# A two-layer hybrid encoder on one core: the delta rule's inverses by smaller blocks stored by row, and roots and gates by ScalarE's logarithm

## The chip, the core and the metric

The kernel runs on one core of one Trainium2 chip. The core has TensorE (matrix products, into PSUM), VectorE and GpSimd (elementwise work and reductions), ScalarE (activation functions, copies with a scale) and SyncE, whose queue starts the transfers of weights. Each engine takes its instructions in order and waits on semaphores for the others. The metric is the device time of one execution in microseconds; the median of three runs before the change is 1150.33 us (1150.1 to 1151.57). Less is better.

## The reference

256 tokens of width 1024 go through two layers. A layer is a gated feed-forward part of width 2752, a mixer and a second feed-forward part, each after an RMS norm; a last norm follows.

```python
for l in range(DEPTH):
    x = x + 0.5 * swiglu(rms_norm(x, ln_ffn1[l]), ffn1_w_in[l], ffn1_w_out[l])
    h = rms_norm(x, ln_mix[l])
    x = x + hybrid_mixer(h, ...)          # window attention, differential attention, gated delta rule
    x = x + 0.5 * swiglu(rms_norm(x, ln_ffn2[l]), ffn2_w_in[l], ffn2_w_out[l])
return rms_norm(x, ln_final)
```

The mixer has six window-attention heads, four differential heads and six heads of a gated delta rule that runs forward and backward over chunks of 64 tokens. For the delta rule each chunk, head and direction needs a triangular solve, and its decay comes from a softplus:

```python
g = -jnp.exp(a_log) * jax.nn.softplus(dn_a + dt_bias)
m_low = where(tril_strict, einsum(kb, kc) * decay, 0)     # 64 x 64
a_mat = eye(64) + m_low
u = triangular_solve(a_mat, vb);  w = triangular_solve(a_mat, kb * exp(gc))
```

With 4 chunks, 6 heads and 2 directions there are 48 unit-triangular matrices of 64 x 64 in a layer. All norms are of the form `v * rsqrt(mean(v*v) + 1e-6)`.

## The kernel before

The state `x` stays on chip with its 1024 channels on partitions, as 8 blocks of 128 x 256 tokens. Feed-forward parts multiply in three passes (`mm3`, L259 to L261): ScalarE splits off a high part of each 128 x 1024 weight block (`load`, L253), VectorE the remainder (L254). The mixer multiplies 32-bit weights directly (`proj`, L428; `token_proj`, L439; `out_proj`, L1024).

The mixer is cut into pieces; the text `ORDER` lists them as they are written into the program. From it the framework plans each engine's queue: it works with priorities in this order and its own idea of when inputs are ready, so the instructions of neighbouring pieces interleave. Weights are fetched on SyncE's queue seven blocks ahead, in the order of the pieces that read them. PSUM has three pools of banks (`BANK`); projections ("pj"), attention scores ("pss"), the gate's projection ("pz") and the output projection ("py") share the two of pool "pm", so a projection or a score waits until a bank has been read out.

The pieces that matter here:

- `N` (`norm`, `norm_scale`): TensorE sums the squares, VectorE forms mean plus EPS (L204), `rsqrt` gives the root, TensorE spreads it over partitions ("pb"). `rsqrt` (L159 to L176) starts from an integer trick and makes three Newton steps, eleven small VectorE instructions. It also serves the feed-forward parts' norms, the q and k norms (`qn`), the differential heads' norm (`dn`), the delta rule's output norm (`on`) and the last norm (`final`).
- `G` (`gates`): beta and g for 24 columns; the softplus term log(1 + e) is a series of 13 VectorE instructions (L466 to L475) after an exponential on ScalarE (L464).
- `c`, `co`, `ce`: nine convolutions, with a Tanh for the SiLU (L559). `qc`, `E`, `X`: decay and the products of k with k and q, into `XE`.
- `ic`, `i`, `ir`, `io`, `ie`: the inverse of the diagonal 32 x 32 blocks. Each partition holds one block; `Vi` and `L` are [128, 32 x 32]. `inv_start` brings the blocks into `L`. One step is a product of broadcast views into `pr` (L799) and a reduction over the last axis (L800). `inv_row` (`ir`) makes rows 1 to 15 of the two 16 x 16 diagonal blocks at once, reading `L` down columns; `inv_off` (`io:0` to `io:5`) makes the 16 x 16 block below. Four of these products, for rows 2, 4, 11 and step 4 (names in `SHARED`: v2, v4, v11, u4), are on GpSimd. `inv_end` transposes the inverse into place; `f` and `g` make the 64 x 64 inverse by products on TensorE.
- `p:9` to `p:16` (`att`), `d` (`diff_scores`), `w` (`win_scores`), `h`, `hw`: projections and attention. A differential head's scores need the maximum on VectorE (L716) and four exponentials on ScalarE (L719) before their two banks are free. They stand between the steps of the inverse in `ORDER`.
- `sa`, `sb`, `sc`: the scan over chunks. `ze`: the output gate, with a Tanh (L927). `on`, `oT`, `o`: output norm, transposes, output projection.

ScalarE's functions come in tables of which one is active; a table load stands in its queue wherever the next function isn't in the active one.

Of the kernel before, what the change touches and what calls it, by code (L numbers as in the profile page):

```python
# [16 lines left out]
P = 128  # L17
# [19 lines left out]
A:0 A:1 A:2 K N A:3 G V c:1:0 c:1:1 clear c:0:0 c:1:2 GS co:1:0 c:0:1 co:1:1 co:1:2 ce:1 GE GT E:1 qn:1 co:0:0 co:0:1  # L37
# [15 lines left out]
SHARED = set("O2 S2 d0 d1 d2 d3 g5 s3 t1 t7 t8 u4 v11 v2 v4 x0 x4 x5".split())  # L53
# [4 lines left out]
class Kernel:  # L58
# [104 lines left out]
    def rsqrt(self, v, n, name, out=None):  # L163

        nc, sp = self.nc, self.sp
        ti = sp.tile([P, n], I32, tag=f"rs_i{n}", name=f"{name}_i")
        nc.vector.tensor_scalar(ti, v.bitcast(I32), 1, None, ALU.arith_shift_right)
        y = sp.tile([P, n], F32, tag=f"rs_y{n}", name=f"{name}_y")
        nc.vector.tensor_scalar(y.bitcast(I32), ti, -1.0, float(0x5F3759DF), ALU.mult, ALU.add)
        a = sp.tile([P, n], F32, tag=f"rs_a{n}", name=f"{name}_a")  # L170
        for i in range(3):
            nc.vector.scalar_tensor_tensor(a, v, -0.5, y, ALU.mult, ALU.mult)
            nc.vector.tensor_tensor(a, a, y, ALU.mult)
            o = y if i < 2 or out is None else out
            nc.vector.scalar_tensor_tensor(o, a, 1.5, y, ALU.add, ALU.mult)
        return o  # L176
# [16 lines left out]
    def norm_scale(self, name, last=False):  # L193
# [12 lines left out]
        self.rsqrt(v, 2, name, rt)  # L206
# [57 lines left out]
    def ffn(self, l, i, gnext, first):  # L264
# [3 lines left out]
        with tc.tile_pool(name=f"hp{nm}", bufs=1) as hp, tc.tile_pool(name=f"ht{nm}", bufs=3) as ht:  # L268
# [19 lines left out]
            for j in range(NF):  # L288
# [34 lines left out]

            c0 = NF * 2048 + 1024
# [30 lines left out]
    def mixer(self, l, gnext):  # L355
# [22 lines left out]
        with ExitStack() as ctx:  # L378
# [74 lines left out]
            def gates():  # L453
# [11 lines left out]
                z1 = tile_([P, 2, 24], "z1")  # L465
                ts(z1, ab, 2.0, None, ALU.add)  # L466
                nc.vector.reciprocal(z1, z1)
                tt(z1, z1, ab, ALU.mult)
                z2 = tile_([P, 2, 24], "z2")
                tt(z2, z1, z1, ALU.mult)  # L470
                sr = tile_([P, 2, 24], "sr")
                ts(sr, z2, 2.0 / 17, None, ALU.mult)
                for m in (15, 13, 11, 9, 7, 5, 3):
                    stt(sr, sr, 2.0 / m, z2, ALU.add, ALU.mult)
                stt(sr, sr, 2.0, z1, ALU.add, ALU.mult)  # L475
# [104 lines left out]
            def qk_norm(a):  # L580

                raw = st["raw", a]
                sqt = tile_([P, 2, 384], "sqt2", "pr")
                act(sqt, raw, AF.Square)
                ss = tile_([P, 12], f"ss{a}")
                nc.vector.tensor_reduce(ss, sqt.rearrange("p t (h d) -> p (t h) d", d=64), AX.X, ALU.add)
                ts(ss, ss, EPS, None, ALU.add)
                rq = self.rsqrt(ss, 12, f"{nm}qk{a}").rearrange("p (t h) -> p t h", t=2)
                if a == 0:
                    ts(rq, rq, 0.125, None, ALU.mult)  # L590
                for p in range(2):
                    v_ = heads6(raw[:, p, :])
                    tt(v_, v_, rq[:, p, :].unsqueeze(2).to_broadcast([P, 6, 64]), ALU.mult)
# [169 lines left out]
            def diff_norm():  # L763
# [6 lines left out]
                r = self.rsqrt(hv, 8, f"{nm}dn").rearrange("p (a h) -> p a h", a=2)  # L770
# [53 lines left out]
            def inv_row(i0, i1):  # L824
                Vi, L = st["Vi"], st["L"]
                for i in range(i0, i1):
                    products(
                        blk(Vi, i, (528, 2), (32, i)),
                        blk(L, i, (528, 2), (0, i), (32, i)),
                        blk(Vi, 0, (528, 2), (32, i), (1, i)),  # L830
                        (2, i, i),
                        True,
                        f"v{i}",
                    )

            def inv_off(n):
                Vi, L, pp = st["Vi"], st["L"], st["pp"]
                if n < 2:
# [3 lines left out]
                        blk(L, 16 + i0, (1, 8), (0, 8), (32, 16)),  # L842
# [175 lines left out]
            def out_proj(part, d):  # L1018
# [20 lines left out]
                "clear": clear, "N": norm, "V": values, "G": gates, "GS": gate_sums, "GE": gate_exps, "GT": gate_rows,  # L1039
                "c": conv, "co": conv_out, "ce": conv_end, "qn": qk_norm, "qc": qk_channels,  # L1040
                "E": decay, "X": products_kq, "K": constants, "p": att, "hw": win_out, "w": win_scores, "d": diff_scores, "h": head_out,
                "dn": diff_norm, "oT": to_oT, "ic": inv_clear, "i": inv_start, "ir": inv_row, "io": inv_off, "ie": inv_end,
# [193 lines left out]
```

## Time and profile before

| what | value |
|---|---|
| median of 3 runs | 1150.33 us |
| profiled execution, its own time | 1153.34 us |
| its span, first to last instruction | 1151.5 us |
| TensorE busy | 1110.3 us, 96% |
| VectorE busy | 738.0 us, 64% |
| ScalarE busy | 522.9 us, 45% |
| GpSimd busy | 82.3 us, 7% |
| mean granted clock of TensorE | 0.977 |
| read from HBM | 171.17 MB |

A share of busy time is a mean over stages with different limits. Matmuls are pipelined and their ends are modelled, so a busy TensorE is not TensorE at its peak: at a lower granted clock the same instructions count as more busy time. In rows of groups the columns are line, engine, operation, result and operands with shapes, count, busy us, mean ns of one, and the idle time before them with what ended it. Rows of the timeline have start, length, engine, line, operation, and in brackets the idle time before and its releaser. PE is TensorE, DVE VectorE, ACT ScalarE, POOL GpSimd, SP SyncE.

### The profile page before, as it was taken

What the parts mean: (1) busy time and instruction counts of PE and PEld (TensorE: products, weight loads), DVE (VectorE), ACT (ScalarE), POOL (GpSimd) and SP (SyncE); (2) the same over time, 40 slices, a digit from 0 to 9 for tenths busy, and PEclk for the clock granted to TensorE, in tenths of its full rate; (3) what the DMA queues carried; (4) which work ended last, traced back from release to release, by engine and by line L of the source; (5) the groups of instructions that cost most, each with busy time, mean ns of one, the idle gap of its engine ahead of it and who ended that gap; (6) DMA issues with size and microseconds to landing.
All of it is one profiled execution on the core that took longest, in us unless ns stands there. A gap on an engine that the chain in (4) does not pass through costs nothing. (4 is left out here: it accounts for less than half of the span.)

```text
span 1151.5 us, 21957 instructions
## 1 busy us (share of the span) xinstructions
PE 1110.3 (96%) x8970; PEld 1022.2 (89%) x8970; DVE 738.0 (64%) x1442; ACT 522.9 (45%) x967; POOL 82.3 (7%) x135
## 2 busy tenths in 40 slices
PE   7999999998899999999999999999988999999996
PEld 7999999776668999999999999988756689999996
DVE  7766654778747566666566666547786476666653
ACT  5545442263472454454444454415436435445441
POOL 0000011101201200000100000121020021000010
PEclk9999999998899999999999999999988999999998
DMA  9655653521123555565555565534211254556521
GB/s 332 213 182 186 201 168 115 164 77 53 51 61 111 198 174 181 184 202 184 181 180 183 182 199 184 161 125 128 79 50 37 75 184 155 185 184 203 184 97 37
DMA packets 49637, 173.64 MB, mean 151 GB/s; under 512 B 5504, under 2 KB 6784, under 8 KB 49536
## 3 DMA queue, kind: packets, MB, share of 16 engines
q1 hardware_dynamic: 49104, 171.64, 45.5%
q8 instruction: 70, 1.15, 0.4%
q10 hardware_dynamic: 432, 0.60, 0.1%
q14 instruction: 31, 0.25, 0.1%
HBM read 171.17 MB, written 1.05 MB: 150 GB/s over the span
## 5 line engine op out<-in xcount | busy, mean ns | idle before, releaser
L254 DVE TENSOR_TENSOR wl<-wr,wh 128x1024 fp32r<-128x1024 f32 x254 | 311.7, 1228 | 172.5 <-ACT wh L253 172.0
L259 PE MATMUL ps<-xh,wh 128*128 128x256 f32 x1336 | 379.6, 284 | 0.8 <-ACT wh L253 0.8
L261 PE MATMUL ps<-xh,wl 128*128 128x256 f32 x1336 | 379.0, 284 | 0.8 <-DVE wl L254 0.8
L253 ACT ACTIVATE wh<-wr 128x1024 fp32r<-128x1024 f32 x254 | 267.2, 1053 | 246.6 <-issue 144.6
L260 PE MATMUL ps<-xl,wh 128*128 128x256 f32 x1336 | 378.7, 283 | 0.0
L259 PEld LDWEIGHTS ps<-xh,wh 128*128 128x128 f32 x1336 | 257.1, 192 | 1.6 <-ACT wh L253 1.0
L261 PEld LDWEIGHTS ps<-xh,wl 128*128 128x128 f32 x1336 | 257.0, 192 | 1.2 <-DVE wl L254 1.2
L260 PEld LDWEIGHTS ps<-xl,wh 128*128 128x128 f32 x1336 | 257.1, 192 | 0.0
L261 PE MATMUL ps<-hh,wl 128*128 128x256 f32 x672 | 187.9, 280 | 0.0
L260 PE MATMUL ps<-hl,wh 128*128 128x256 f32 x672 | 187.7, 279 | 0.0
L259 PE MATMUL ps<-hh,wh 128*128 128x256 f32 x672 | 187.6, 279 | 0.0
L428 PE MATMUL pj<-xf,wr 128*128 128x256 f32 x544 | 133.6, 402 | 2.9 <-issue 2.6
L260 PEld LDWEIGHTS ps<-hl,wh 128*128 128x128 f32 x672 | 126.3, 188 | 0.0
L261 PEld LDWEIGHTS ps<-hh,wl 128*128 128x128 f32 x672 | 126.1, 188 | 0.0
L259 PEld LDWEIGHTS ps<-hh,wh 128*128 128x128 f32 x672 | 125.9, 187 | 0.0
L428 PEld LDWEIGHTS pj<-xf,wr 128*128 128x128 f32 x544 | 107.6, 203 | 20.0 <-issue 3.3
L191 POOL TENSOR_TENSOR sqacc<-sqacc,sqt 128x256 f32<-128x256 f32 x41 | 34.6, 843 | 733.0 <-ACT sqt L187 732.9
L282 ACT ACTIVATE hh<-h 128x256 fp32r<-128x256 f32 x88 | 36.1, 416 | 90.4 <-DVE h L280 90.4
L277 DVE TENSOR_TENSOR t<-ps,f_rb 128x256 f32<-128x256 f32 x88 | 36.9, 424 | 37.9 <-PE ps L261 37.7
L1024 PE MATMUL py<-oT,wr 128*128 128x256 f32 x256 | 58.9, 384 | 0.0
L283 DVE TENSOR_TENSOR hl<-h,hh 128x256 fp32r<-128x256 f32 x88 | 36.8, 423 | 30.5 <-ACT hh L282 30.5
L1024 PEld LDWEIGHTS py<-oT,wr 128*128 128x128 f32 x256 | 47.2, 190 | 7.0 <-DVE x L1031 0.4
(321 smaller groups left out, 1128.5 us busy)
## 6 DMA issues: line engine op xcount, KB each, us to landing
wr<-in_ffn SPq DMA_DIRECT2D x258, 512.0 KB, 3.4
wr<-in_mix SPq DMA_DIRECT2D x50, 512.0 KB, 3.5
wr<-in_mix SPq DMA_DIRECT2D x8, 408.0 KB, 3.2
wr<-in_mix SPq DMA_DIRECT2D x8, 384.0 KB, 3.0
x<-in_x SPq DMA_DIRECT2D x4, 256.0 KB, 4.1
ar<-in_ffn SPq DMA_DIRECT2D x8, 128.0 KB, 3.9
cb<-in_constb SPq DMA_DIRECT2D x1, 588.0 KB, 10.1
out_y<-fo SPq DMA_DIRECT2D x2, 256.0 KB, 2.4
```

What stands on the lines that cost most here:

```text
L191: (eng or nc.gpsimd).tensor_tensor(self.sq, self.sq, t, ALU.add)
L253: nc.scalar.activation(h, w, AF.Copy)
L254: nc.vector.tensor_tensor(lo, w, h.bitcast(F32), ALU.subtract)
L259: mm(out, lhsT=ah, rhs=bh, start=start, stop=False)
L260: mm(out, lhsT=ah, rhs=bl, start=False, stop=False)
L261: mm(out, lhsT=al, rhs=bh, start=False, stop=stop)
L277: nc.vector.tensor_tensor(t[:rows], gate, rb[:rows], ALU.mult)
L282: nc.scalar.activation(hh[:n, j, :], h[:n], AF.Copy)
L283: nc.vector.tensor_tensor(hl[:n, j, :], h[:n], hh[:n, j, :].bitcast(F32), ALU.subtract)
L428: mm(ps[:, 0:S], lhsT=w[:, k * P : (k + 1) * P], rhs=xf[:, k, :], start=k == 0, stop=k == KD - 1)
L1024: mm(ps[:, 0:S], lhsT=st["o", q // NBLK][:, c], rhs=oT[:, k, :], start=k == ks[0], stop=k == ks[-1])
```

## The change

- **Inverse.** `ir` makes only rows 1 to 7, of four 8 x 8 diagonal blocks at once. Four new steps `im:0` to `im:3` (`inv_mid`) make the 8 x 8 block below each pair: per 16 x 16 block one step for L times the upper inverse into `pp`, one for the lower inverse times that. `io:0` to `io:5` stay, with `io:0` to `io:2` reading `L` by rows.
- **Layout.** `inv_start` transposes on VectorE the four groups that ScalarE copied before, and copies the other four, so that `L` is stored by row where it was stored by column.
- **GpSimd.** v2, v4, v11 and u4 leave `SHARED`: every product of the inverse is on VectorE.
- **Roots.** `rsqrt` takes `exp(-0.5 * ln(v))` on ScalarE and one Newton step on VectorE in the mixers' first norm, the output norm and the last norm; the feed-forward norms, `qn` and `dn` keep the old form.
- **Softplus.** `ln(1 + e)` is one activation on ScalarE in place of the series.
- **Tables.** `log_table` puts a load of the table with logarithm and exponential at the head of each mixer (`lt`), after `ze`, and in the last feed-forward part after its last hidden block. The load is queued behind the ScalarE instruction written before it.
- **Order.** `ORDER` loses `ir:8:9` to `ir:15:16` and gains `im:0` to `im:3` and the two `lt`.

```diff
-ir:3:4 ir:4:5 ir:5:6 p:15 ir:6:7 ir:7:8 ir:8:9 ir:9:10 ir:10:11 ir:11:12 ir:12:13 ir:13:14 c:2:2 ir:14:15 p:14 p:13
-co:2:0 p:16 d:0 ir:15:16 d:2 co:2:1 io:0 co:2:2 p:9 d:1 p:12 d:3 w:0 io:1 h:2 h:1 p:10 h:0 io:2 io:3 h:3 p:11 w:1 w:2
+ir:3:4 ir:4:5 ir:5:6 p:15 ir:6:7 ir:7:8 im:0 im:1 im:2 c:2:2 im:3 p:14 p:13 co:2:0 p:16 d:0 d:2 co:2:1 io:0 co:2:2 p:9
+d:1 p:12 d:3 w:0 io:1 h:2 h:1 p:10 h:0 io:2 io:3 h:3 p:11 w:1 w:2 hw:0 io:4 io:5 ie ce:2 dn hw:1 f g:0 hw:2 g:1 sa:0
...
-SHARED = set("O2 S2 d0 d1 d2 d3 g5 s3 t1 t7 t8 u4 v11 v2 v4 x0 x4 x5".split())
+SHARED = set("O2 S2 d0 d1 d2 d3 g5 s3 t1 t7 t8 x0 x4 x5".split())
...
-    def rsqrt(self, v, n, name, out=None):
+    def rsqrt(self, v, n, name, out=None, log=True):
...
+        if log:
+            nc.scalar.activation(y, v, AF.Ln)
+            nc.scalar.activation(y, y, AF.Exp, scale=-0.5)
+        else:
...
-        for i in range(3):
+        steps = 1 if log else 3
+        for i in range(steps):
...
+    def log_table(self):
+
+        self.tc.keep_in_program_order(self.nc.scalar.preload_act_table_set("natural_log_exp_and_others"))
...
-                    _, rb = self.norm_scale(nm)
+                    _, rb = self.norm_scale(nm, log=False)
...
+            if gnext is None:
+                self.log_table()
...
-                z1 = tile_([P, 2, 24], "z1")
-                ts(z1, ab, 2.0, None, ALU.add)
-                nc.vector.reciprocal(z1, z1)
-                tt(z1, z1, ab, ALU.mult)
-                z2 = tile_([P, 2, 24], "z2")
-                tt(z2, z1, z1, ALU.mult)
                 sr = tile_([P, 2, 24], "sr")
-                ts(sr, z2, 2.0 / 17, None, ALU.mult)
-                for m in (15, 13, 11, 9, 7, 5, 3):
-                    stt(sr, sr, 2.0 / m, z2, ALU.add, ALU.mult)
-                stt(sr, sr, 2.0, z1, ALU.add, ALU.mult)
+                act(sr, ab, AF.Ln, bias=1.0)
...
-                        if (b < 2) == (v == 0):
+                        if (b < 2) != (v == 0):
                             nc.vector.transpose(o_, XE[B32[b], 0, us, B32[b % 2]])
...
-                        blk(Vi, i, (528, 2), (32, i)),
-                        blk(L, i, (528, 2), (0, i), (32, i)),
-                        blk(Vi, 0, (528, 2), (32, i), (1, i)),
-                        (2, i, i),
+                        blk(Vi, i, (264, 4), (32, i)),
+                        blk(L, 32 * i, (264, 4), (0, i), (1, i)),
+                        blk(Vi, 0, (264, 4), (32, i), (1, i)),
+                        (4, i, i),
...
+            def inv_mid(n):
+
+                Vi, L, pp = st["Vi"], st["L"], st["pp"]
+                a, step = n % 2, n // 2
+                if step == 0:
+                    products(
+                        blk(pp, a * 64, (1, 8), (8, 8)),
+                        blk(L, a * 528 + 8 * 32, (32, 8), (0, 8), (1, 8)),
+                        blk(Vi, a * 528, (0, 8), (32, 8), (1, 8)),
+                        (8, 8, 8), False, f"m{n}",
+                    )
+                else:
+                    products(
+                        blk(Vi, a * 528 + 8, (1, 8), (32, 8)),
+                        blk(Vi, a * 528 + 264, (1, 8), (0, 8), (32, 8)),
+                        blk(pp, a * 64, (0, 8), (8, 8), (1, 8)),
+                        (8, 8, 8), True, f"m{n}",
+                    )
...
-                        blk(L, 16 + i0, (1, 8), (0, 8), (32, 16)),
+                        blk(L, (16 + i0) * 32, (32, 8), (0, 8), (1, 16)),
...
-                        blk(L, 16 + 8 * 32, (1, 16), (0, 8), (32, 8)),
+                        blk(L, 16 * 32 + 8, (32, 16), (0, 8), (1, 8)),
```

More of the change, by code (lines that the diff above doesn't have):

```diff
@@ L160, in psum @@
         return self.pools[tag].tile(shape, F32, tag=tag, name=name)
-    def rsqrt(self, v, n, name, out=None):
+    def rsqrt(self, v, n, name, out=None, log=True):
         nc, sp = self.nc, self.sp
-        ti = sp.tile([P, n], I32, tag=f"rs_i{n}", name=f"{name}_i")
-        nc.vector.tensor_scalar(ti, v.bitcast(I32), 1, None, ALU.arith_shift_right)
         y = sp.tile([P, n], F32, tag=f"rs_y{n}", name=f"{name}_y")
-        nc.vector.tensor_scalar(y.bitcast(I32), ti, -1.0, float(0x5F3759DF), ALU.mult, ALU.add)
+        if log:
+            nc.scalar.activation(y, v, AF.Ln)
+            nc.scalar.activation(y, y, AF.Exp, scale=-0.5)
+        else:
+            ti = sp.tile([P, n], I32, tag=f"rs_i{n}", name=f"{name}_i")
+            nc.vector.tensor_scalar(ti, v.bitcast(I32), 1, None, ALU.arith_shift_right)
+            nc.vector.tensor_scalar(y.bitcast(I32), ti, -1.0, float(0x5F3759DF), ALU.mult, ALU.add)
         a = sp.tile([P, n], F32, tag=f"rs_a{n}", name=f"{name}_a")
-        for i in range(3):
+        steps = 1 if log else 3
+        for i in range(steps):
             nc.vector.scalar_tensor_tensor(a, v, -0.5, y, ALU.mult, ALU.mult)
             nc.vector.tensor_tensor(a, a, y, ALU.mult)
-            o = y if i < 2 or out is None else out
+            o = y if i < steps - 1 or out is None else out
             nc.vector.scalar_tensor_tensor(o, a, 1.5, y, ALU.add, ALU.mult)
@@ L191, in sq_add, with norm_scale @@
                 (eng or nc.gpsimd).tensor_tensor(self.sq, self.sq, t, ALU.add)
-    def norm_scale(self, name, last=False):
+    def log_table(self):
+        self.tc.keep_in_program_order(self.nc.scalar.preload_act_table_set("natural_log_exp_and_others"))
+    def norm_scale(self, name, last=False, log=True):
         nc = self.nc
@@ L827, in inv_row @@
                     products(
-                        blk(Vi, i, (528, 2), (32, i)),
-                        blk(L, i, (528, 2), (0, i), (32, i)),
-                        blk(Vi, 0, (528, 2), (32, i), (1, i)),
-                        (2, i, i),
+                        blk(Vi, i, (264, 4), (32, i)),
+                        blk(L, 32 * i, (264, 4), (0, i), (1, i)),
+                        blk(Vi, 0, (264, 4), (32, i), (1, i)),
+                        (4, i, i),
                         True,
                         f"v{i}",
+                    )
[7 more added lines that the diff above has]
+                        blk(Vi, a * 528, (0, 8), (32, 8), (1, 8)),
+                        (8, 8, 8),
+                        False,
+                        f"m{n}",
+                    )
[4 more added lines that the diff above has]
+                        blk(pp, a * 64, (0, 8), (8, 8), (1, 8)),
+                        (8, 8, 8),
+                        True,
+                        f"m{n}",
                     )
@@ L1038, in mixer @@
             pieces = {
-                "clear": clear, "N": norm, "V": values, "G": gates, "GS": gate_sums, "GE": gate_exps, "GT": gate_rows,
+                "clear": clear, "lt": self.log_table, "N": norm, "V": values, "G": gates, "GS": gate_sums, "GE": gate_exps, "GT": gate_rows,
                 "c": conv, "co": conv_out, "ce": conv_end, "qn": qk_norm, "qc": qk_channels,
                 "E": decay, "X": products_kq, "K": constants, "p": att, "hw": win_out, "w": win_scores, "d": diff_scores, "h": head_out,
-                "dn": diff_norm, "oT": to_oT, "ic": inv_clear, "i": inv_start, "ir": inv_row, "io": inv_off, "ie": inv_end,
+                "dn": diff_norm, "oT": to_oT, "ic": inv_clear, "i": inv_start, "ir": inv_row, "im": inv_mid, "io": inv_off, "ie": inv_end,
                 "f": off1, "g": off2, "ze": gate_out, "sa": scan_a, "sb": scan_b, "sc": scan_c, "on": out_norm, "o": out_proj,
```

13 lines of the change are left out of this document (6 added, 7 removed).

## The prediction

> **What bounds the kernel now.** I read the page first, then windows of the two mixers, then the groups, waits and timeline of the stage where TensorE falls short of its pace.
>
> ```profile
> span 1151.5 us, 21957 instructions
> PE 1110.3 (96%) x8970; PEld 1022.2 (89%) x8970; DVE 738.0 (64%) x1442; ACT 522.9 (45%) x967; POOL 82.3 (7%) x135
> ```
>
> TensorE is busy 96% of the span, so at most some 40 us can be had unless a stage runs at a lower clock. The windows view shows such a stage once in each layer, around the inverse (columns: window, its length, PE, PEld, DVE, ACT, POOL busy with counts, granted clock, DMA).
>
> ```profile
> 257.00:310.00 53.00, 44.10 (x167) 31.76 (x167) 45.06 (x84) 20.31 (x61) 10.67 (x9) 0.84 0.15 50
> 820.00:873.00 53.00, 43.91 (x168) 31.66 (x169) 45.03 (x84) 19.81 (x58) 10.65 (x9) 0.84 0.16 50
> ```
>
> The layers agree within 0.2 us. VectorE works 45 of 53 us, and TensorE runs at a granted clock of 0.84. What VectorE's other time is shows in its groups for 261 to 310 us:
>
> ```profile
> L799 DVE TENSOR_TENSOR pr<-L,Vi 128x1024 f32<-128x1024 f32 (+12 forms) x15 | 11.6, 775 | 0.2
> L800 DVE TENSOR_REDUCE Vi<-pr 128x64 f32<-128x1024 f32 (+16 forms) x18 | 8.5, 472 | 5.5 <-POOL pr L799 5.3
> L716 DVE TENSOR_REDUCE mxd<-pss 128x2 f32<-128x512 f32 x8 | 5.5, 687 | 1.5 <-PE pss L713 1.5
> L799 DVE TENSOR_TENSOR pr<-Vi,pp 128x1024 f32<-128x1024 f32 x2 | 3.9, 1940 | 0.0
> L800 DVE TENSOR_REDUCE pp<-pr 128x64 f32<-128x1024 f32 (+1 forms) x3 | 3.6, 1214 | 0.0
> ```
>
> The inverse takes 11.6 + 8.5 + 3.9 + 3.6 = 27.6 us of VectorE per layer, and 5.3 us more stand idle for the products on GpSimd. Only about 2 us wait for TensorE. So 50 of the 53 us are VectorE's own queue: it sets the pace here. How that reaches TensorE shows at the largest wait of its list (us in total, times, longest) and in the timeline of layer 0:
>
> ```profile
> PE pss L675 <- ACT sc L719: 8.0, 2, 4.0
> ```
>
> ```profile
> 297.49 3.69 POOL L799 TENSOR_TENSOR pr<-Vi,pp 128x1024 f32<-128x1024 f32 x1
> 301.22 1.22 DVE L800 TENSOR_REDUCE Vi<-pr 128x64 f32<-128x1024 f32 x1 [3.98 <-POOL pr L799]
> 302.35 0.68 DVE L716 TENSOR_REDUCE mxd<-pss 128x2 f32<-128x512 f32 x1
> 303.13 0.47 ACT L719 ACTIVATE sc<-pss,mxd 128x256 f32<-128x256 f32 x1 [4.02 <-DVE mxd L716]
> 304.20 2.07 PE L675 MATMUL pss<-wq 64*128 64x256 f32 x4 [4.00 <-ACT sc L719]
> 307.97 6.18 PE L428 MATMUL pj<-xf,wr 128*128 128x256 f32 x16
> ```
>
> GpSimd's 3.69 us product holds VectorE 3.98 us; queued behind it is the maximum of the last differential head; ScalarE's exponentials wait for that, and TensorE waits 4.00 us for their bank. Then a projection, 16 instructions, takes 6.18 us.
>
> **The change part by part.**
>
> *Inverse.* Three things set its cost: how many elements, at what rate, and where. The rate now depends on how L and Vi are read:
>
> ```profile
> L277 DVE TENSOR_TENSOR t<-ps,f_rb 128x256 f32<-128x256 f32 x84 | 35.2, 424 | 36.7 <-PE ps L261 36.5
> L254 DVE TENSOR_TENSOR wl<-wr,wh 128x1024 fp32r<-128x1024 f32 x254 | 311.7, 1228 | 172.5 <-ACT wh L253 172.0
> L799 DVE TENSOR_TENSOR pr<-L,Vi 128x1024 f32<-128x1024 f32 x6 | 12.1, 2022 | 0.0
> L799 DVE TENSOR_TENSOR pr<-L,Vi 128x450 f32<-128x450 f32 x2 | 1.8, 913 | 0.1
> L799 DVE TENSOR_TENSOR pr<-L,Vi 128x2 f32<-128x2 f32 x2 | 0.3, 142 | 0.0
> L800 DVE TENSOR_REDUCE Vi<-pr 128x30 f32<-128x450 f32 x2 | 1.2, 616 | 0.0
> ```
>
> Products of contiguous operands cost (1228 - 424)/768 = 1.05 ns an element; those with L read down a column, 32 elements apart, (913 - 142)/448 = 1.72. Reductions cost (1214 - 616)/574 = 1.04. Floors are 0.14 and 0.15 us. After, L is read along its rows in row steps, the first half of the middle steps and io:0 to io:2, so I price these at 1.05; the second half of the middle steps still reads Vi 32 apart (1.72), and io:3 to io:5 are as now. Seven rows of 4i² elements, 560 in all: products 7 x 0.142 + 0.59 = 1.58, reductions 1.60, together 3.2 us. Four middle steps of 512 elements: 2 x (0.68 + 0.68) + 2 x (1.02 + 0.68) = 6.1. io:0 to io:2: 3 x (1.23 + 1.21) = 7.3. io:3 to io:5, all on VectorE: 3 x (1.94 + 1.21) = 9.5. Sum 26.1 us, against 27.6 + 5.3 = 32.9: 6.8 us less of VectorE's queue per layer, most of it the vanished wait. The other end: if short rows bring nothing, rows, middle steps and io:0 to io:2 cost 0.4, 0.7 and 2.4 more, 29.5 in all, and 3.4 us are saved. I take 6.8, since the operands will then look like L254's. At full clock TensorE needs about 35 us of these 53 (five projections at 3.62 make 18.1, eight score banks at 1.35 make 10.8, the rest 6), so VectorE stays the bound and its gain passes on.
>
> ```profile
> 280.97 6.05 PE L428 MATMUL pj<-xf,wr 128*128 128x256 f32 x16
> 291.22 3.62 PE L428 MATMUL pj<-xf,wr 128*128 128x256 f32 x16
> 300.00:310.00 10.00, 6.00 (x18) 4.62 (x19) 8.77 (x13) 4.11 (x15) 2.45 (x2) 0.64 0.00 0
> ```
>
> *Clock.* Two of the projections here take 6.05 and 6.18 us where the same work takes 3.62; the clock around the second is 0.64. With the 4.00 us stall cut to about half (1.94 us of product on VectorE in its place) the second may run fast: 2.5 us. I take half, 1.2 per layer; the ends are 0 and, for both, 5.0.
>
> [...] But the 6.05 us projection comes after idle stretches of 1.5 us at most, which speaks for less than the whole.
>
> *Gates and norm at the mixer's head.* The softplus loses 13 VectorE instructions (L466 to L475) for one logarithm:
>
> ```profile
> L474 DVE SCALAR_TENSOR_TENSOR sr<-sr,z 128x48 f32<-128x48 f32 x14 | 2.9, 208 | 0.5
> L467 DVE RECIPROCAL z<-z 128x48 f32<-128x48 f32 x2 | 0.9, 453 | 0.1
> L464 ACT ACTIVATE ab<-ab 128x48 f32<-128x48 f32 x2 | 0.5, 243 | 0.0
> PE ptr L412 <- DVE cs L571: 2.6, 4, 1.2
> PE pkq L412 <- DVE raw L593: 1.8, 2, 0.9
> ```
>
> That is 7 x 0.208 + 0.453 + 5 x 0.2 = 2.9 us of VectorE against 0.24 of ScalarE, just ahead of the convolutions. TensorE then waits for VectorE (2.6 + 1.8)/2 = 2.2 us per layer; VectorE also waits for ScalarE and for projections there, so I take 1.0 (ends 0 and 2.2). The change adds a wait of VectorE for the logarithm; queued behind it are the first convolution's pads, which need their projection until about 213 us anyway, and ScalarE has nothing between the exponential of ab and that convolution's first tap. The norm's root saves about 1 us, but the gates also need the last of A:3 on TensorE, so I count nothing for it. The output norm's two roots lie under the 50 output-projection instructions ("py", 11 us) and count nothing; without that cover they would save 1 us each.
>
> No transfer is added or moved: weights are fetched in the order of the pieces that read them, and that order stays.
>
> *Final norm.* It is the end of the chain:
>
> ```profile
> 1141.46 0.17 DVE fin_v L204
> ...
> 1143.62 0.17 DVE fin_r L175
> 1143.84 1.24 PE fin_pb L209 x4
> L524 ACT ACTIVATE egl<-egl 128x24 f32<-128x24 f32 x2 | 0.4, 206 | 0.0
> ```
>
> Eleven instructions at a pitch of 0.195 take 2.15 us. After: two activations of 0.21 with 0.04 of handover, then three of 0.195, 1.05 in all: 1.1 us less.
>
> *Tables.* Loads now number six: one at the start, two at L460, three at L278 for the feed-forward parts' Silu. After, each mixer has one for the logarithm, one for the first Tanh, one more for the logarithm; with the final norm's that is five more, 1.28 us each:
>
> ```profile
> L460 ACT ACT_TABLE_LOAD x2 | 2.6, 1283 | 0.0
> 199.20 1.28 ACT L460 ACT_TABLE_LOAD   x1
> 200.50 0.21 ACT L460 ACTIVATE ea<-row 128x12 f32<-128x12 f32 x1
> 217.30 0.42 ACT L559 ACTIVATE th<-pad 128x256 f32<-128x256 f32 x1 [2.68 <-DVE pad L550]
> 357.52 0.49 ACT L968 ACTIVATE SC<-px 128x384 f32<-128x384 f32 x1 [5.81 <-DVE SC L967]
> ```
>
> The first of a mixer replaces the one at 199.20; the first Tanh has 2.68 us idle before it; after the gate's Tanh ScalarE idles 5.81 us; in the last feed-forward part it is half idle. All five are hidden, so nothing is counted; with that cover gone they cost 6.4 us.
>
> [...] Here 0.02 us lie between the load's end and the next activation, so I keep 1.28.
>
> *Sum.* Per layer 6.8 + 1.2 + 1.0 = 9.0; two layers 18.0; final norm 1.1: 19.1 us. The profiled execution took 1153.34 us (span 1151.5 and 1.8 around it), 3.0 over the median of 1150.33. 1153.3 - 19.1 = 1134.2, in terms of the runs 1131.
>
> **The rivals.**
>
> More: both slow projections recover (5.0) and the head gains 2.2: 2 x (6.8 + 5.0 + 2.2) + 1.1 = 29.1, 1121. For it: the clock row of 0.64. Against: TensorE still idles a quarter of the stage.
>
> Less: rows of eight elements are no faster than columns. 2 x 3.4 + 1.1 = 7.9 and no clock gain, 1142. For it: the runs are only 1 to 16 elements long, and no such row is in the trace.
>
> Table loads on the path: 1131 + 6.4 = 1137.6. For it: ScalarE serves its queue in order and the planner places the activations anew. Against: the idle times above.
>
> [...]
>
> No change: TensorE's two score banks, passed between three engines, set the pace, and VectorE's freed time becomes waiting; only the final norm's 1.1 is left, 1149. Against: 2 us of such waiting in 53.
>
> Slower: the GpSimd waits cost nothing, since the maximum behind them would have come late anyway, and the strided price stays. Then VectorE has 29.5 us of inverse instead of 27.6 in a stage that it bounds: 1150.3 + 2 x 1.9 - 1.1 = 1153. It decides once the products of L and Vi stay near 1.7 ns an element and the end of the stage doesn't move though the wait is gone. Against: the 4.00 us follow the 3.98 step by step.
>
> **How the numbers follow.** Chances: forecast 0.5 (own range 1124 to 1138), more 0.13, less 0.14, tables 0.10 (0.01 of it by the page's figure), no change 0.06, slower 0.07. About 0.2%, 2.3 us, is what a measurement can tell. Faster 0.87, the same 0.06, slower 0.07. The range 1120 to 1146 takes in the ends of the unknown costs and leaves out the last two cases.
>
> **What would show each step.** Right: no wait of L800 for GpSimd; the product of 1024 elements of L and Vi near 1.23 us; the stage from L's transpose to the last Vi 6 to 8 us shorter; the wait of pss for sc under half of 4.00; the projection after it near 3.6 us; eleven table loads with no wait of TensorE behind them; the final chain 1.1 us shorter. Wrong: that product still near 2 us, VectorE idle for TensorE by several us more in the stage, or more than eleven loads, which would mean that logarithms and Tanhs alternate.

## The result, and the profile after

The changed kernel takes 1142.81 us (median; 1139.94 to 1143.54) against 1150.95 for the kernel before in the same session: a ratio of 0.992, 95% interval 0.9906 to 0.9933, 8.1 us less. The forecast was 1131 us, 19 less. The profiled execution took 1143.04 us, span 1141.3, only 0.2 over its median, where that of before lay 2.4 over its own; between the two profiles lie 10.3 us.

First VectorE's groups with their shapes, of the changed kernel (its lines 803 and 804 are 799 and 800 of before):

```profile
L803 DVE TENSOR_TENSOR pr<-Vi,pp 128x1024 f32<-128x1024 f32 x6 | 12.1, 2021 | 0.0
...
L803 DVE TENSOR_TENSOR pr<-L,Vi 128x1024 f32<-128x1024 f32 x6 | 7.3, 1212 | 0.0
...
L803 DVE TENSOR_TENSOR pr<-Vi,pp 128x512 f32<-128x512 f32 x4 | 4.1, 1036 | 0.1
...
L803 DVE TENSOR_TENSOR pr<-L,Vi 128x512 f32<-128x512 f32 x4 | 2.8, 692 | 0.1
```

The prices are those forecast: 1212 ns by rows (2022 by columns before), 692 and 1036 for the middle steps (0.68 and 1.02). ScalarE's group of the new table loads, of the changed kernel:

```profile
L202 ACT ACT_TABLE_LOAD x5 | 6.4, 1283 | 0.1
```

and TensorE's waits there (us in total, times, longest):

```profile
PE pss L712 <- ACT sc L723: 3.0, 2, 1.5
...
PE pss L679 <- ACT sc L723: 1.4, 2, 0.7
```

Five more loads, no wait of TensorE for one. The 4.00 us stall per layer (8.0 in two) is 0.7 (1.4). But VectorE's stage, from L's transpose to the last write of Vi, has become shorter by much less than the 6 to 8 us that the prediction names as its sign. Before (layer 0):

```profile
261.50 1.23 DVE L820 STREAM_TRANSPOSE L<-Dg 128x1024 f32<-128x1024 f32 x1
...
306.25 1.21 DVE L800 TENSOR_REDUCE Vi<-pr 128x64 f32<-128x1024 f32 x1
```

and after:

```profile
260.10 1.24 DVE L824 STREAM_TRANSPOSE L<-Dg 128x1024 f32<-128x1024 f32 x1
...
302.38 1.21 DVE L804 TENSOR_REDUCE Vi<-pr 128x64 f32<-128x1024 f32 x1
```

The stage takes 43.5 us where it took 46.0; in layer 1 43.8 against 45.9. What the change is worth to TensorE show the two mixers (windows view, TensorE's part: window, length, PE busy, PEld busy, and the granted clock third from the end). Of the kernel before:

```profile
197.59:389.24 191.65, 179.83 (x1362) 136.72 (x1360) 134.27 (x359) 87.46 (x234) 27.96 (x51) 0.95 0.30 97
761.84:952.64 190.80, 179.44 (x1362) 136.48 (x1360) 132.53 (x359) 87.43 (x234) 27.75 (x43) 0.95 0.30 97
```

and of the changed one:

```profile
197.40:381.37 183.97, 175.84 (x1362) 133.72 (x1361) 127.65 (x318) 91.52 (x243) 24.47 (x47) 0.97 0.31 101
756.30:942.28 185.98, 179.03 (x1362) 136.53 (x1360) 126.32 (x318) 91.92 (x243) 24.14 (x39) 0.95 0.31 100
```

The mixers are 7.7 and 4.8 us shorter, and the final norm's chain 1.1. Together that makes 13.6 us, and the profiles are only 10.3 apart: the feed-forward parts are 3.3 us longer. Their groups, before:

```profile
L259 PE MATMUL ps<-xh,wh 128*128 128x256 f32 x1336 | 379.6, 284 | 0.8 <-ACT wh L253 0.8
...
L261 PE MATMUL ps<-hh,wl 128*128 128x256 f32 x672 | 187.9, 280 | 0.0
L260 PE MATMUL ps<-hl,wh 128*128 128x256 f32 x672 | 187.7, 279 | 0.0
L259 PE MATMUL ps<-hh,wh 128*128 128x256 f32 x672 | 187.6, 279 | 0.0
```

and after:

```profile
L270 PE MATMUL ps<-xh,wh 128*128 128x256 f32 x1336 | 379.2, 284 | 0.6 <-ACT wh L264 0.6
...
L272 PE MATMUL ps<-hh,wl 128*128 128x256 f32 x672 | 190.3, 283 | 0.0
L271 PE MATMUL ps<-hl,wh 128*128 128x256 f32 x672 | 190.3, 283 | 0.0
L270 PE MATMUL ps<-hh,wh 128*128 128x256 f32 x672 | 190.3, 283 | 0.0
```

Code that the change doesn't touch: the matmuls on hh and hl, the output half, take as long as those on xh and xl now. The mean lengths of 279 to 284 ns overlap; from start to start the matmuls are 120.0 ns apart (the "pitch" from here on), before 117.8: 2016 x 2.2 ns = 4.4 us. A stretch at half clock (granted clock 0.50) of 3.4 us, from 16.1 us on, which the profile of before has in its first feed-forward part and that of the changed kernel hasn't, takes 1.7 us off again. What moved is where hh and hl lie. The new root needs no integer tile; with the last one of six columns gone, hh is, by the framework's layout of the tiles, at byte 123360 of its partition instead of 123424, 64 lower, and hl likewise. No trace shows addresses; the next runs test them by their effect.

### The profile page after: what moved, and what is told of

Its sections match the earlier page's. It is cut to its first block, busy times and chain, and to the rows that moved or that the text cites. A ratio compares the mean times of both kernels' runs of the same rounds, so it can differ in the third digit from the quotient of the medians.

```text
span 1141.3 us, 21887 instructions
## 1 busy us (share of the span) xinstructions
PE 1109.4 (97%) x8970; PEld 1022.8 (90%) x8970; DVE 723.7 (63%) x1352; ACT 533.2 (47%) x988; POOL 75.4 (7%) x127
## 4 chain that ended last, share of the span: by engine, by line
PE 84%; DVE 7%; issue 4%; ACT 3%; DMA 1%; POOL 0%; SPq 0%; DVEq 0%; ACTq 0%; POOLq 0%
PE ps L272 21%; PE ps L270 21%; PE ps L271 21%; PE py L1052 5%; PE pj L441 5%; PE pz L452 2%; PE pv L452 2%; DVE pr L803 1%; PE pss L717 1%; DVE pad L554 1%; DVE wl L265 1%; PE pso L754 1%; PE px L973 1%; DVE mxd L720 1%; DVE Vi L804 1%
## 5 line engine op out<-in xcount | busy, mean ns | idle before, releaser
L272 PE MATMUL ps<-hh,wl 128*128 128x256 f32 x672 | 190.3, 283 | 0.0
L271 PE MATMUL ps<-hl,wh 128*128 128x256 f32 x672 | 190.3, 283 | 0.0
L270 PE MATMUL ps<-hh,wh 128*128 128x256 f32 x672 | 190.3, 283 | 0.0
L441 PE MATMUL pj<-xf,wr 128*128 128x256 f32 x544 | 130.8, 396 | 2.8 <-issue 2.8
L270 PEld LDWEIGHTS ps<-hh,wh 128*128 128x128 f32 x672 | 129.1, 192 | 0.0
L272 PEld LDWEIGHTS ps<-hh,wl 128*128 128x128 f32 x672 | 129.1, 192 | 0.0
L271 PEld LDWEIGHTS ps<-hl,wh 128*128 128x128 f32 x672 | 129.1, 192 | 0.0
## 6 DMA issues: line engine op xcount, KB each, us to landing
cb<-in_constb SPq DMA_DIRECT2D x1, 588.0 KB, 10.2
```

The source lines that it names most:

```text
L270: mm(out, lhsT=ah, rhs=bh, start=start, stop=False)
L271: mm(out, lhsT=ah, rhs=bl, start=False, stop=False)
L272: mm(out, lhsT=al, rhs=bh, start=False, stop=stop)
L441: mm(ps[:, 0:S], lhsT=w[:, k * P : (k + 1) * P], rhs=xf[:, k, :], start=k == 0, stop=k == KD - 1)
```

## Experiments: the pitch of the feed-forward matmuls

Addresses modulo 256 in the changed kernel: wh and wl 224, xh and xl 224, hh and hl 224; before, hh and hl had 32. Distances below are from weight to moving operand, modulo 256; the 256 is my choice, and no run tests it against another modulus.

**The changed kernel again.** No edit.

> The changed kernel as it is, once more. In its first profile the matmuls of the output half of the feed-forward parts (moving operand hh or hl) started 120.0 ns apart, in the kernel before 117.8 ns; and layer 1's mixer gained 1.9 us less of the whole (4.8 against 7.7) than layer 0's. If the pitch is a state of the chip, it may be 117.8 here; if it comes from where hh and hl lie in SBUF (64 bytes lower than before, since a small tile is gone), it is 120.0 again. If layer 1's smaller gain is a matter of how the granted clock happens to fall, the mixers' two spans lie elsewhere by 1 us or more while the sum of the kernel stays within 1140 to 1144.

1143.07 us, ratio 0.9927 (0.9915 to 0.9939), pitch 120.0 again in both halves. The mixers took 183.84 and 185.89, as in the first profile, so this execution doesn't tell whether layer 1's smaller gain is chance; the mixers of the later kernels do.

**hh and hl moved back.**

```
+            hp.tile([P, 16], F32, name="gap")
             hh = hp.tile([P, NF + 1, S], F32R, name="hh")
```

> The changed kernel with 64 unused bytes ahead of hh in the feed-forward pool, so that hh and hl lie where they lay in the kernel before. Theory (address): the output-half matmuls go back to 117.8 ns apart, 2016 x 2.2 ns = 4.4 us less, some 1138 us. Rival (state of the chip, or the new order of work): pitch as in the run of the changed kernel beside it, time within 1 us of it.

1135.21 us, ratio 0.9862 (0.9848 to 0.9877); pitch 117.8. It is 7.9 us under the run beside it, where 4.4 were expected. Against the changed kernel's first profile, 7.4 us longer, the feed-forward parts give 4.8, the mixers (183.97 and 183.94) 2.0, the final norm's two small matmuls, at half clock in the changed kernel's profile, 0.5.

**All four moved.**

```
         self.x = self.xp.tile([P, KD, S], F32, tag="x", name="x")
+        self.xp.tile([P, 16], F32, name="gap")
```

> The changed kernel with 64 unused bytes between x and xh, so that xh, xl, hh and hl all lie 32 bytes past a multiple of 256, where hh and hl lay in the kernel before (xh and xl lay 224 past it in both). Theory (address): the input-half matmuls, 120.0 ns apart in both kernels, fall to 117.8 as well: about 4100 x 2.2 ns = 9 us on top of the 4.4, some 1129 us. Rival (the input half is slower for another reason, its weights or its order): as the run with hh and hl alone, 1138, or with no effect of addresses at all 1143.

1111.09 us, with executions from 1101.2 to 1120.7 (ratio, without the longest, 0.9631, 0.9599 to 0.9663): far more than expected. The counts of matmuls per 100 us show why. The changed kernel, third feed-forward part:

```profile
600.00:700.00 100.00, 100.00 (x835) 100.00 (x835) 65.14 (x90) 48.25 (x73) 0.00 (x0) 1.00 0.59 189
```

and the kernel with all four moved, its second and third part:

```profile
400.00:500.00 100.00, 100.00 (x852) 100.00 (x851) 65.60 (x90) 48.77 (x71) 0.00 (x0) 1.00 0.60 195
600.00:700.00 100.00, 100.00 (x884) 100.00 (x883) 67.91 (x93) 49.77 (x73) 0.74 (x1) 1.00 0.60 200
```

At the same granted clock of 1.00 the pitch is 120.0, 117.8 or 113.4 ns; in this execution it went from the second to the third at the seam of the second and third part and stayed. All 6024 matmuls at 117.8 or all at 113.4 are 26.5 us apart, which would be enough for the spread; only this one execution has a profile.

**Gaps of different sizes in each part.**

```
+            g0, g1 = ((8, 16), (32, 16), (16, 24), (56, 8))[2 * l + i - 1]
+            hp.tile([P, g0], F32, name="gap0")
             hh = hp.tile([P, NF + 1, S], F32R, name="hh")
+            hp.tile([P, g1], F32, name="gap1")
```

> The changed kernel with gaps of different sizes ahead of hh and of hl in each of the four feed-forward parts, so that the offsets of their rows past a multiple of 256 bytes are 0 and 64, 96 and 160, 32 and 128, 192 and 224. Theory (address): the pitch of the matmuls differs with the offset, 117.8 at 32 and 120.0 at 224, and the others tell the rule (a row that begins 32 past a multiple of 128, say, would be fast at 32 and 160). Rival (state): one pitch everywhere.

1136.36 us (one execution). All four output halves had a mean pitch of 117.7 to 117.9, also where hl lay at 224; single matmuls varied from 113 to 122. Offset 224, which all four operands have in the changed kernel at 120.0, isn't slow by itself, and a rule by offset alone falls.

**Weights moved along with the rest.**

```
         warm = cp.tile([P, 1], F32, name="warm")
+        cp.tile([P, 16], F32, name="gap")
```

> The changed kernel with 64 unused bytes ahead of all the weight buffers, so that wh and wl (stationary) move by 64 bytes together with xh, xl, hh and hl (moving): all lie 32 bytes past a multiple of 256, and as to one another as in the changed kernel, where all lay 224 past. Theory (the distance between the stationary and the moving operand counts): pitch 120.0 ns everywhere, 1143 us. Rival (the place of the moving operand itself counts): 117.8 or 113.3 as in the kernel with xh, xl, hh and hl moved alone, 1101 to 1121 us.

1143.42 us, ratio 0.9937 (0.9924 to 0.995), 120.0 everywhere. Here hh, hl, xh and xl lie exactly where the kernel with all four moved has them, and that one takes 1111: what counts is the distance to the weights.

**Distances of 128 and of 32** (the gap of the third kernel with 32 or with 8 elements).

> The changed kernel with 128 unused bytes between x and xh: the moving operands lie 96 past a multiple of 256, the weights 224, a distance of 128 modulo 256 (64 in the kernel with 64 bytes). Theory (any distance other than 0 modulo 256 is as good as 64, as the gaps of different sizes suggest, whose output halves all ran at 117.8): 117.8 or 113.3, 1101 to 1121 us. Rival (only a distance that isn't a multiple of 128 helps): 120.0, 1143 us. If the spread of the kernel with 64 bytes comes from a switch of the pitch in the middle of an execution, the runs spread here too.

> The changed kernel with 32 unused bytes between x and xh, so that the moving operands lie at a multiple of 256 and the weights 224 past one: a distance of 32 modulo 256 (64: 117.8 or 113.3 ns; 128: 118.9 ns; 0: 120.0 ns). If the pitch falls as the distance departs from 0 modulo 256 in either way, some 117 to 119 ns here as well, 1125 to 1140 us; if a fixed gap of at least 64 bytes is needed, 120.0 and 1143.

Distance 128: 1136.13 us, ratio 0.9878 (0.9859 to 0.9897), pitch 118.4 to 119.8. Distance 32: 1121.92 us, ratio 0.974 (0.9726 to 0.9754), pitch 116 to 119, executions within 1121.2 to 1124.8. Of the four distances modulo 256, 0 is the worst (120.0 ns, 1143 us), and 64 the best and least steady (117.8 or 113.4 ns, 1101.2 to 1120.7 us).

## Experiments: what the mixers' gain consists of

**The inverse alone, the logarithms alone**, each put into the kernel before, with hh and hl where they lay there.

> The kernel before with the inverse of the changed kernel alone (blocks of 8 by 8, L stored by row, all products on VectorE); roots, softplus and table loads as before; hh and hl lie as in the kernel before. Theory: the inverse gives the most of the mixers' gain: of the 183.9 us that a mixer takes in the changed kernel with hh and hl moved back (before: 191.6 and 190.8), all but the head's 1.0, so some 185 us in each layer, 12.5 us less in sum and about 1138. Rival (the gain is in the head and the new tables only move work about): under 6 us, 1145 or more.

> The kernel before with the logarithms alone (roots of the mixers' norm, of the output norm and of the final norm, softplus, and the five table loads more); the inverse as before; hh and hl put where they lay before by 64 unused bytes, since a small tile of the old root is gone. Theory: 2 x 1.0 at the mixers' heads and 1.1 in the final norm, 3.1 us, 1147.5. Rival (tables reach the path): 1150 or more, with a wait for ScalarE of 1 us or more behind a load.

Inverse alone: 1140.47 us, ratio 0.9901 (0.9888 to 0.9914), 10.8 less where 12.5 were expected; mixers 187.29 and 183.50. Logarithms alone: 1148.71, ratio 0.9981 (0.9969 to 0.9993), 2.5 less where 3.1 were expected; the final norm's chain is 1.1 shorter and the tables wait nowhere. Together 13.3 us, near the 15.4 of both with hh and hl moved back. That kernel was run once more as a ground for the later ones (fourth row of the table below), with 1133 to 1139 us and mixers of 182 to 187 expected: 1135.96 us, 16.2 less than the kernel before beside it, mixers 185.95 and 182.68.

But the inverse's two layers, one code, differ by 3.8 us. So I split each mixer's length by windows of 1 us: TensorE's idle time, the time at half clock (twice what the granted clock lacks of 1.00, summed) and the rest, which is the length less the idle time and less half of the time at half clock. Here is such a stretch, the second one of layer 1 in the changed kernel:

```profile
855.00:856.00 1.00, 0.74 (x4) 0.21 (x2) 1.00 (x2) 0.60 (x3) 0.00 (x0) 1.00 0.00 0
856.00:857.00 1.00, 0.53 (x1) 0.49 (x2) 0.98 (x3) 0.91 (x3) 0.00 (x0) 0.61 0.00 0
857.00:858.00 1.00, 1.00 (x4) 0.67 (x2) 1.00 (x5) 0.55 (x2) 0.00 (x0) 0.50 0.00 0
...
862.00:863.00 1.00, 1.00 (x4) 0.77 (x3) 1.00 (x3) 0.33 (x3) 0.00 (x0) 0.50 0.00 0
863.00:864.00 1.00, 1.00 (x6) 0.90 (x5) 0.58 (x2) 0.33 (x1) 0.00 (x0) 0.98 0.00 0
```

The clock lacks 0.39 + 6 x 0.50 + 0.02 = 3.41 us: 6.8 us at half clock. Layer 0, the same instructions, has no such stretch there.

| kernel | layer 0: length, idle, half clock, rest | layer 1 |
|---|---|---|
| before | 191.65, 11.8, 20.5, 169.6 | 190.80, 11.4, 20.5, 169.2 |
| after | 183.97, 8.1, 10.2, 170.7 | 185.98, 6.9, 17.1, 170.5 |
| after, hh and hl back | 183.97, 6.9, 13.7, 170.2 | 183.94, 7.0, 13.6, 170.2 |
| the same again | 185.95, 6.9, 17.0, 170.6 | 182.68, 8.2, 6.8, 171.1 |
| inverse alone | 187.29, 8.1, 17.1, 170.7 | 183.50, 7.4, 10.2, 171.0 |
| logarithms alone | 189.66, 9.7, 20.4, 169.8 | 190.47, 10.6, 20.4, 169.7 |
| before, four products to VectorE | 190.29, 9.9, 20.5, 170.2 | 186.86, 9.2, 13.7, 170.8 |
| io:0 to io:2 twice | 183.61, 8.9, 10.3, 169.6 | 183.65, 8.9, 10.2, 169.7 |
| the same again | 189.68, 8.9, 23.9, 168.9 | 183.64, 8.9, 10.2, 169.6 |
| L by column | 186.73, 8.0, 17.0, 170.2 | 187.30, 7.5, 20.5, 169.6 |
| io:3 to io:5 left out | 183.03, 7.3, 10.2, 170.6 | 182.65, 6.7, 10.2, 170.9 |
| two projections moved ahead | 188.28, 8.5, 23.9, 167.9 | 188.19, 8.2, 23.9, 168.1 |

The time at half clock comes in multiples of 3.41 us (2 to 7 of them), and the rest is 168 to 171 us in all of them. This only divides the length, and doesn't say why TensorE idles: a mixer is some 170 us of TensorE's own work, and what varies is its idle time and the number of such steps. Equal code gets 2 steps in one layer and 5 in the other. A step costs up to 1.7 us, less where part of it lies in idle time: in the second run of io:0 to io:2 twice, four steps and 6.0 us lie between the layers at equal idle time, 1.5 each.

Within an execution all stretches of both layers begin on one grid: in the kernel before at 275.49, 302.80, 838.69 and 865.99 us, the last three 8, 165 and 173 times 3.413 us behind the first. The two executions of the changed kernel have this grid in the same place (first stretch at 272.54 and 272.51) and the same steps; the two with hh and hl back have it elsewhere (270.85 and 272.48) and different steps. The first stretch of each layer of the changed kernel begins during or just behind an idle time of 1.5 us; with L by column one begins at 855.78 us, although TensorE has been busy without a gap since 847.0:

```profile
847.00:848.00 1.00, 1.00 (x5) 0.64 (x4) 1.00 (x1) 0.58 (x4) 0.00 (x0) 1.00 0.27 107
...
854.00:855.00 1.00, 1.00 (x6) 0.66 (x4) 1.00 (x2) 0.61 (x3) 0.64 (x1) 1.00 0.83 336
855.00:856.00 1.00, 1.00 (x8) 0.55 (x6) 1.00 (x1) 0.73 (x4) 0.00 (x0) 0.89 0.01 4
856.00:857.00 1.00, 1.00 (x3) 0.81 (x3) 1.00 (x3) 0.20 (x1) 0.00 (x0) 0.50 0.00 0
```

Part of what runs there are the differential heads' scores, which use 32 rows where the projections use 128 (`dqk 32*128` and `xf,wr 128*128` in the timelines). If each matmul's time, to the start of the next at most, is weighted by its share of 128 rows, the intervals of the grid from 100 to 1000 us of all 18 traces fall apart like this. Of those at full clock, all 46 with a weighted share under 0.46 are followed by half clock, none of 4365 over 0.64, and 16 of the 189 between. Of those at half clock, 83 of 85 under 0.80 are followed by another, and 60 of 67 over it by full clock. That is a pattern found in the traces afterwards; no run was made to test it.

**GpSimd's four products to VectorE**, nothing else.

```
-SHARED = set("O2 S2 d0 d1 d2 d3 g5 s3 t1 t7 t8 u4 v11 v2 v4 x0 x4 x5".split())
+SHARED = set("O2 S2 d0 d1 d2 d3 g5 s3 t1 t7 t8 x0 x4 x5".split())
```

> The kernel before with the four products of the inverse that GpSimd had (u4, v2, v4, v11) on VectorE and nothing else changed: the waits of the reductions for GpSimd, 5.3 us per layer, are gone, and VectorE gets 1.94 + 0.14 + 0.2 + 0.55 us of products instead, 2.8: its queue is 2.5 us shorter per layer. Forecast's step (VectorE's queue sets the pace, its gain passes on whole): 5 us less in sum, 1145.5, or some 2 more if the projection behind the 4.00 us stall recovers its clock. Rival (the freed time becomes waiting for TensorE): within 1.5 us of the kernel before.

1145.07 us, ratio 0.9948 (0.9936 to 0.996): 6.2 less, the size that the forecast's step gives. More than half of what the whole new inverse brings comes from this one line. By its profile it is 1.9 and 2.2 us less idle time, and two steps of half clock in layer 1. But the mixers are 1.4 and 3.9 us shorter, not 2.5 each, and VectorE's stage from L's transpose to the last Vi takes 46.6 and 45.7 us, as before (46.0 and 45.9). So the agreement in the sum is in part luck and doesn't show that VectorE's queue sets the pace.

**VectorE's time added.** The products of io:0 to io:2 are made twice.

```
             def inv_off(n):
+                if n < 3:
+                    inv_off_once(n)
+                inv_off_once(n)
+
+            def inv_off_once(n):
```

> The changed kernel with hh and hl moved back (1135.2 us) and the three first products of the inverse's last part (io:0, io:1, io:2, a product of 1.21 us and a reduction of 1.21 each) done twice with the same result: 7.3 us more of VectorE in each layer's stage. Theory of the forecast (VectorE sets the pace there): 14.6 us more in sum, some 1150. Rival (TensorE sets it now, VectorE has slack): under 7 us more, below 1142; what passes on tells the share.

> The kernel with io:0 to io:2 done twice, once more, beside its ground: 7.3 us more of VectorE per layer. Its first profile had the mixers at 183.6, its runs lay from 1135.7 to 1146.1. If VectorE's time passes on through the clock alone, a slower execution's mixers have more steps at half clock (17 to 24 us instead of 10.2) and the same rest of about 170 us; if it passes on by waits, TensorE's idle time is larger instead. Median 5 to 9 us over the ground either way; if under 3, VectorE's time is free there.

1142.77 us (1135.7 to 1146.1) and again 1140.76 (1135.6 to 1147.7), against 1135.21 and 1135.96 without: 7.6 and 4.8 us in the medians, of 14.6 added; the first lies between the theory and its rival. The two profiles show how. In the first, of its fastest execution, 7.3 us more of VectorE per layer cost nothing (183.61, 183.65); in the second one layer is 6 us longer at equal idle time:

```profile
196.10:385.78 189.68, 180.80 (x1362) 137.90 (x1361) 131.49 (x324) 91.94 (x243) 23.17 (x47) 0.94 0.30 98
758.34:941.98 183.64, 174.73 (x1362) 133.23 (x1361) 131.61 (x324) 91.85 (x243) 22.71 (x39) 0.97 0.31 101
```

Length less PE busy is 8.9 us in both rows; the clock differs, 0.94 and 0.97, four steps.

**L by column again**, in the changed kernel with hh and hl back. The five reads of L swap their strides, the transposes in inv_start their side:

```
-                        blk(L, 32 * i, (264, 4), (0, i), (1, i)),
+                        blk(L, i, (264, 4), (0, i), (32, i)),
```

> The changed kernel with hh and hl moved back (1135.2 us), with L stored by column as in the kernel before (the block scheme, the short rows and VectorE's share unchanged): products of L and Vi of 1024 elements take 2.02 us again instead of 1.21, VectorE has some 3.8 us more per layer. Forecast's rival ('less', VectorE sets the pace): 7.6 us more, some 1143. What the doubled products suggest (VectorE has slack there): the mixers stay at 184 but for steps of 1.7 us of half clock, 1134 to 1139.

1141.96 us, ratio 0.992 (0.9906 to 0.9933): 6.8 us more, against the 7.6 of the forecast's rival; my expectation of 1134 to 1139 was wrong. So VectorE's time passes on nearly whole here, where the doubled products passed on a third to a half. By the profile, of its slowest execution, it does so by the clock again: there are three to four steps more in the two layers together than in the two profiles without the edit, and 0.5 us more idle time per layer.

**VectorE's time taken away.** io:3 to io:5 return at once, so this kernel leaves out a block of the inverse and doesn't compute the encoder.

> The changed kernel with hh and hl moved back and the last three products of the inverse with their reductions left out (io:3, io:4, io:5, so that the block of the inverse that couples the two halves of 16 is missing): 9.5 us less of VectorE per layer. The forecast's step (VectorE sets the pace and what it gains passes on): 19 us less, 1116. Rival (TensorE sets the length of a mixer by its own work, 170 us, its idle time and half of its time at half clock): 3.5 to 10 us less, for at most two or three steps of 1.7 us per layer and an idle us; mixers of 179 to 183.

1134.01 us, ratio 0.9837 (0.9825 to 0.985): 1.9 us less, where VectorE's pace would have given 19, and less than the rival's 3.5 to 10 too. Its timeline shows what is still there (the fence gives start, duration, engine, line, and in brackets the idle time before):

```profile
269.76 0.44 PE L426 MATMUL ptr<-cst,cs 128*128 128x128 f32 x2
271.73 0.59 PE L713 MATMUL pss<-ddb,sdiag 128*128 128x512 bf16 x1 [1.53 <-ACT sc L724]
272.25 2.07 PE L718 MATMUL pss<-dqk 32*128 32x256 f32 x4
274.25 0.61 PE L713 MATMUL pss<-ddb,sdiag 128*128 128x512 bf16 x1
274.78 2.07 PE L718 MATMUL pss<-dqk 32*128 32x256 f32 x4
276.78 5.80 PE L442 MATMUL pj<-xf,wr 128*128 128x256 f32 x16
```

1.53 us for ScalarE's exponentials, and the projection at half clock behind it. The maximum that the exponentials need starts on VectorE at 269.93, 0.1 us behind the end of the scores, so the inverse's instructions ahead of it have next to no part in this wait.

**Work put into that idle time**, on the kernel with all four operands moved.

```
-                ps = bank("pj")
+                ps = self.psum([P, 512], "pj", "pd" if i in (9, 12) else "pm")
-... d:0 d:2 co:2:1 io:0 co:2:2 p:9 d:1 p:12 d:3 ...
+... d:0 p:9 d:2 co:2:1 io:0 co:2:2 p:12 d:1 d:3 ...
```

> The kernel with 64 bytes between x and xh (1101 to 1121 us), with the projections p:9 and p:12 put ahead of the second and third differential head's scores and given banks of the other group, so that TensorE has work where it idled 1.5 us for the exponentials, just ahead of its first stretch at half clock. Read per mixer, since the feed-forward parts' pitch differs between executions. Theory (that idle time brings the half clock; a mixer takes some 170 us plus its idle time plus half of its time at half clock, which came in steps of 3.41 us): no such stretch in the 20 us behind it, idle time 1.5 us less; from 182.8 and 184.2 us to 178 to 181. Rival (the half clock comes from elsewhere): two to five steps remain, 182 or more.

The mixers are longer, 188.28 and 188.19 with seven steps of half clock each; in all 1117.71 us, with executions from 1114.5 to 1135.4 (ratio, without the longest, 0.9707, 0.9684 to 0.973). The order around it changed as well, so this shows that the edit doesn't help, not what brings the half clock; that stays open.

## Why the prediction was wrong

Against the forecast's 19.1 us the profiles show 10.3, and the medians 8.1.

- *Prices of the inverse's instructions, GpSimd's wait gone, table loads hidden, final norm 1.1*: right, each instruction and the norm within 0.1 us; in sum the inverse takes 26.4 us of VectorE per layer where 26.1 were priced. A table load takes 1283 ns here, with no wait of TensorE; behind the one after layer 0's `ze`, from 347.17 to 348.45 us, the next activation starts 0.02 us later. The figure to which the prediction gives 0.01 of its chances for tables is shown by no run.
- *Head, 1.0 per layer*: from the first value projection to L's transpose 1.2 and 0.6. Right.
- *"VectorE stays the bound and its gain passes on"*: this is the step that failed. VectorE's queue did become some 6.5 us shorter per layer, but 2.1 us (layer 0) and 2.5 (layer 1) of that came back as waits for TensorE. Up to the last Vi VectorE stands idle 3.6 and 4.0 us for scores (pss) and projections (pj), before 1.5 in each layer; the rows are below, and this is a sign of being wrong that the prediction names. Another 2.1 us of the stage are other VectorE work that now runs earlier, so the stage shows 2.5 and 2.1 us. TensorE's idle time shrank by 3.7 and 4.4 us, the head's share included, instead of 6.8 and the head's 1.0. The prediction compared TensorE's 35 us at full clock with VectorE's 50, but its own row says that at the clock it had TensorE was busy 44.1 of the 53 us. Idle were 8.9, a sixth and not the quarter that the prediction puts against "more"; beyond these, VectorE's gain could reach TensorE only by the clock. How much of VectorE's time passes on has no single share in these runs: 9.5 us less per layer gave 1.9 of 19, 7.3 more cost a third to a half, and L by column cost 6.8 of 7.6.

```profile
275.86 0.69 DVE L720 TENSOR_REDUCE mxd<-pss 128x2 f32<-128x512 f32 x1 [0.87 <-PE pss L717]
...
278.40 0.69 DVE L720 TENSOR_REDUCE mxd<-pss 128x2 f32<-128x512 f32 x1 [0.52 <-PE pss L717]
...
284.25 0.42 DVE L663 SCALAR_TENSOR_TENSOR wq<-pj,m_rb 128x256 f32<-128x256 f32 x1 [1.38 <-PE pj L441]
...
285.52 0.69 DVE L720 TENSOR_REDUCE mxd<-pss 128x2 f32<-128x512 f32 x1 [0.85 <-PE pss L717]
...
834.61 0.69 DVE L720 TENSOR_REDUCE mxd<-pss 128x2 f32<-128x512 f32 x1 [0.72 <-PE pss L717]
...
837.15 0.69 DVE L720 TENSOR_REDUCE mxd<-pss 128x2 f32<-128x512 f32 x1 [0.52 <-PE pss L717]
...
843.51 0.42 DVE L663 SCALAR_TENSOR_TENSOR wq<-pj,m_rb 128x256 f32<-128x256 f32 x1 [1.89 <-PE pj L441]
...
844.78 0.69 DVE L720 TENSOR_REDUCE mxd<-pss 128x2 f32<-128x512 f32 x1 [0.85 <-PE pss L717]
```

- *Clock, 1.2 per layer (0 to 5.0)*: the direction was right, the size not, and the cause isn't shown: the stall fell to 0.7 us in both layers, but the second stretch at half clock vanished in layer 0 alone. Six steps became three in layer 0 and five in layer 1, worth at most 5.1 and 1.7 us. The sum of 9.0 per layer thus came out at 7.7 in layer 0 by two errors that offset each other (3.7 of idle time and 5.1 of half clock, less 1.1 by which the rest grew), and at 4.8 in layer 1 (4.4 and 1.7, less 1.3). Over the two profiles with hh and hl back the mean is 7.1 per layer.
- *Feed-forward parts unchanged*: wrong by 3.3 us net in the profiles (4.4 by the pitch, less the 1.7 of the stretch at 16 us, plus 0.6 of other differences). The prediction had this term at nothing, and said only that no transfer is added or moved. What hh and hl would do elsewhere, the profile of before doesn't show; 120.0 and 117.8 ns stood side by side in it for two halves of the same code, and I didn't ask why.
- *3.0 us between profile and median*: 2.4 in the later runs of before, 0.2 after. An offset of one execution doesn't carry over: 2.2 us.

Shortfall: mixers 5.5, feed-forward 3.3, offset 2.2, in sum 11.0 = 19.1 - 8.1. Of the rivals, "less" came closest in time (1142) for a reason that doesn't hold, since rows were as fast as forecast; "no change" had the right idea, VectorE's freed time becoming waiting, but too much of it. With hh and hl put back the change is worth 15.4 us and takes 1135.2; that this is within 4 us of the forecast is luck in part, since the idle time gave less than forecast and the clock more.

## What to carry to other kernels

Before an engine's saved time is counted whole, work out the same stage for the next engine with its idle and slow-clock time in it; where both stand near the limit, a saving passes on only until the second one binds, as the 1.9 us for 9.5 per layer show. That doesn't make added time free: in two of these kernels it came back as steps of half clock. When an edit removes or resizes a tile, look at where the later tiles of SBUF land: here 64 bytes between weights and moving operand, modulo 256, were worth more than the whole change: the changed kernel takes 1111 us with them, 1143 without (1122, and steadier, with 32). And compare per-stage rows of untouched code first: they show such a shift at once.

## What the runs showed of the hardware

- The pitch of the feed-forward matmuls (256 columns, weights loaded for each) went with the distance of their moving operand from their weights in SBUF: 120.0 ns at 0 modulo 256 bytes, 116 to 119 at 32, 117.8 or 113.4 at 64, 118.4 to 119.8 at 128, at a granted clock of 1.00 in all. It is no matter of single matmuls: in the fourth part of the kernel with different gaps hl was at distance 0, hh at 224, and the mean over its output half was 117.8. Why, and why 64 has two, is open.
- TensorE's half clock (granted clock 0.50) came in steps of 3.41 us on one grid per execution, 2 to 7 of them in a mixer, and equal code got different numbers (5 and 2 in the two layers of the second run with hh and hl back). One stretch began with no idle time in the 8.8 us ahead of it (at 855.78 us with L by column). In the 18 traces the share of busy time weighted by the rows in use sorts nearly all intervals at full clock (under 0.46 half clock followed in 46 of 46, over 0.64 in none of 4365); that this share is the cause is not shown.
